# Routed experts in an order found on the chip, in pairs of a small and a large count, with slab addresses from registers

## The chip, the cores and the metric

The kernel runs on one core of a Trainium2 chip. The metric is device time in microseconds, the median of several runs. The engines are TensorE (PE in the profile, with PEld for its weight loads), VectorE (DVE), ScalarE (ACT), GpSimd (POOL) and SyncE (SP); 16 DMA engines move data for all of them.

## The reference

One decoder layer on 512 tokens of 1024 features, in float32. Three sub-layers follow each other, each with a residual and a layer norm: a gated token mixer (mLSTM and latent attention), a cross-attention into 256 memory tokens, and a mixture of experts. Only the last matters here:

```python
logits = xt @ w_router + b_router            # 512 x 32
top_val, top_idx = lax.top_k(logits, 4)      # four experts per token
gate = jax.nn.softmax(top_val)
# for each expert e, for its tokens only:
gu = x @ w_gu[e] + b_gu[e]                   # 1024 -> 2048
h  = clamped_swiglu(gu)                      # 1024
y += gate * (h @ w_dn[e] + b_dn[e])          # 1024 -> 1024
```

There are 32 experts and 2048 assignments, 64 per expert on average. Every expert has 12 MB of weights (8 MB in `w_gu`, 4 MB in `w_dn`), and every expert's weights are read once.

## The kernel before, in words

The dense part (mixer, cross-attention, router) takes the first third of the time. While its last token blocks are finished, `router_block` computes for each block of 128 tokens the logits, the top four, a 0/1 mask `M`, each token's place in its expert's list `pm` (1, 2, 3, ..., 0 where it isn't routed), the gates `G`, and for each expert the columns `VT` with the token number and the gate in bfloat16 parts. `router_end` sums the mask to the counts.

`experts` then runs over e = 0 to 32 in the order of the experts' numbers, software-pipelined over three experts at once. In iteration e TensorE does the up projection of expert e in four quarters (`up`), turns the hidden rows of expert e-1 behind the first quarter (`hidden`), makes the slot list of expert e+2 behind the third (`route_expert`), does the two halves of the down projection of expert e-1 (`down`), and between those halves turns the gathered tokens of expert e+1 (`tokens`). The order of TensorE, VectorE, ScalarE and GpSimd within this loop is written out by hand (`manual_schedule`); each engine works through its list in order.

The tokens are the stationary operand and the weights stream. What an expert costs TensorE goes by its count: 64 tokens always, 32 more if it passes 64, again 32 if it passes 96, and 64 more if it passes 128 (up to 192; beyond that `overflow`). Each of these is a branch on a register that TensorE, VectorE, ScalarE and GpSimd load from the expert's count (`number`, `conds`, line 1233). The results lie in PSUM tiles `gu` (four buffers) and `y` (two). Those of `down` use the same buffers: `y`, `y2` from `y`, and `y3`, `yx` from `gu`; `rows_out` copies them out, first the ones beyond 128, then 96 to 128, 64 to 96, and the first 64, and scatters the rows with addition into `based` in DRAM (line 1017).

The weights come as slabs of 128 x 1024 floats, 24 per expert: 16 for up, 8 for down. They go through a ring of 36 buffers. SyncE issues all of them in a fixed list (`order`, lines 1246 to 1249): up of e, then down of e-1. The first 36 are issued while the router ends; after each up projection 16 more are queued in SyncE's list, after each down projection 8 more. A slab waits on SyncE until its buffer, that of the slab 36 before, has been used.

GpSimd makes the one-hot matrix of an expert's slots from `pm` (`one_hots`, line 984), one expert ahead of its slot list, and does the gathers and scatters. The bias rows are added by a bfloat16 matmul with a selection matrix `esel`, whose column e picks expert e's row.

The lines around which the change is made:

```python
        order = []
        for e in range(33):
            order += [(e, h, k) for k in range(8) for h in range(2) if e < 32]
            order += [(e - 1, 2, k) for k in range(8) if e]
```

Of the kernel before, what the change touches and what calls it, by code (L numbers as in the profile page):

```python
# [9 lines left out]
F32 = mybir.dt.float32  # L10
F32R = mybir.dt.float32r
BF = mybir.dt.bfloat16
I32 = mybir.dt.int32
U32 = mybir.dt.uint32
AF = mybir.ActivationFunctionType
OP = mybir.AluOpType
AX = mybir.AxisListType
# [92 lines left out]
class Trunk:  # L110
# [772 lines left out]
    def router_init(self):  # L883
        nc, p, a = self.nc, self.route, self.a
        self.wr = p.tile([128, 8, 32], F32, name="wr")
        nc.gpsimd.dma_start(self.wr, a["wr"])
        self.br = p.tile([128, 32], F32, name="br")
        nc.gpsimd.dma_start(self.br, a["br"].to_broadcast([128, 32]))
        self.io32 = p.tile([128, 32], F32, name="io32")
        nc.gpsimd.iota(self.io32, pattern=[[1, 32]], base=0, channel_multiplier=0, allow_small_or_imprecise_dtypes=True)  # L890
        io = self.t2("placesf", [CAP])
        nc.gpsimd.iota(io, pattern=[[1, CAP]], base=1, channel_multiplier=0, allow_small_or_imprecise_dtypes=True)
        self.places = p.tile([128, CAP], BF, name="places")
        nc.vector.tensor_copy(self.places, io)
        self.tri = p.tile([128, 128], BF, name="tri")
        nc.vector.tensor_scalar(self.tri, self.ij, 0.0, None, op0=OP.is_gt)
        self.onesb = p.tile([128, 128], BF, name="onesb")
        nc.vector.memset(self.onesb, 1.0)
        self.M = p.tile([128, 4, 32], BF, name="M")
        self.pm = p.tile([128, 4, 32], F32, name="pm")  # L900

        self.VT = p.tile([128, 4, 32, 8], BF, name="VT")
        self.G = p.tile([128, 4, 32], F32, name="G")
        nc.gpsimd.memset(self.VT, 0.0)
        pid = p.tile([128, 1], F32, name="pid")
        nc.gpsimd.iota(pid, pattern=[[0, 1]], base=0, channel_multiplier=1, allow_small_or_imprecise_dtypes=True)
        for b in range(4):
            nc.gpsimd.tensor_copy(self.VT[:, b, :, 0], pid.to_broadcast([128, 32]))
            nc.gpsimd.memset(self.VT[:, b, :, 1], 128.0 * b - NONE)

        self.esel = p.tile([128, 32], BF, name="esel")
        e = p.tile([128, 32], F32, name="eself")
        for i in range(4):
            nc.gpsimd.iota(e[32 * i:32 * i + 32], pattern=[[1, 32]], base=0, channel_multiplier=-1,
                           allow_small_or_imprecise_dtypes=True)
        nc.vector.tensor_scalar(self.esel, e, 0.0, None, op0=OP.is_equal)
        nc.vector.memset(self.esel[96:128], 0.0)

    def router_block(self, b, x2):
# [46 lines left out]
    def router_end(self):  # L966

        nc, p = self.nc, self.route
        pc = self.ps("pc", "tp")
        for b in range(4):  # L970
            nc.tensor.matmul(pc[:, :32], self.onesb, self.M[:, b], start=b == 0, stop=b == 3)
        self.countf = p.tile([128, 32], F32, name="countf")
        nc.vector.tensor_copy(self.countf, pc[:, :32])
        self.count = p.tile([1, 32], I32, name="count")
        nc.vector.tensor_copy(self.count, pc[0:1, :32])
        self.most = p.tile([1, 1], I32, name="most")
        m = p.tile([1, 1], F32, name="mostf")
        nc.vector.reduce_max(m, pc[0:1, :32], axis=AX.X)
        nc.vector.tensor_copy(self.most, m)

    def one_hots(self, e, pool):
        oh = pool.tile([128, 4, CAP], BF, name="oh", tag="oh", bufs=1)
        for b in range(4):
            self.nc.gpsimd.tensor_scalar(oh[:, b], self.places, self.pm[:, b, e:e + 1], None, op0=OP.is_equal)  # L984
        return oh

    def route_expert(self, e, pool, oh, bank="tp"):
# [244 lines left out]
    def cond(self, c, *engines):  # L1232
        return self.nc.values_load(c[0:1, 0:1], engines=engines, min_val=0, max_val=512,
                                   skip_runtime_bounds_check_because="a count of the 512 tokens")

    def experts(self):
        nc, tc, a = self.nc, self.tc, self.a
        p, cond = self.mx, self.cond
        PE, DVE, ACT, POOL = (mybir.EngineType.PE, mybir.EngineType.DVE, mybir.EngineType.Activation, mybir.EngineType.Pool)
        self.more_x = p.tile([64, 1024], F32, name="mrxg", bufs=1)  # L1240
        nc.gpsimd.memset(self.more_x, 0.0)
        self.ys = [p.tile([128, 1024], F32, name=f"ysb{i}", bufs=1) for i in range(2)]
        for y in self.ys:
            nc.gpsimd.memset(y, 0.0)
# [5 lines that stand above are left out]
        slabs, self.nfetch = {}, 0  # L1250

        def fetch(n):

            for e, part, k in order[self.nfetch:self.nfetch + n]:
                slabs[e, part, k] = self.slab(a["wdn"][e, k] if part == 2 else a["wgu"][e, part, k])
            self.nfetch += n

        def number(e):

            c = self.mx.tile([1, 1], I32, name="number", tag="number", bufs=4)  # L1260
            nc.gpsimd.tensor_copy(c, self.count[0:1, e:e + 1])
            return c

        def conds(c):
            return cond(c, PE, ACT), cond(c, DVE, ACT), cond(c, POOL), cond(c, PE)

        def more_gather(e):
            with tc.If(rv[e][2] > 128):
                self.gather(self.more_x, route[e][1][0])

        def routing(e):
            route[e] = self.route_expert(e, self.mx, self.oh)
            if e < 31:
                count[e + 1] = number(e + 1)
                self.oh = self.one_hots(e + 1, self.mx)

        count = {0: number(0), 1: number(1)}
        route, rv, h = {0: self.first}, {0: conds(count[0])}, {}
        self.bias_rows()
        fetch(len(self.ring["s"][0]))  # L1280
        more_gather(0)
        xs, ls = {0: self.tokens(rv[0][0])}, {}
        self.oh = self.one_hots(1, self.mx)
        with tc.manual_schedule(engines={PE, DVE, ACT, POOL}):
            routing(1)
            rv[1] = conds(count[1])
            self.gather(self.xg, route[1][0][0])
            more_gather(1)
            for e in range(33):
                f = e - 1  # L1290

                def turn_units():
                    if 0 < e < 33:
                        h[f] = self.hidden(rv[f][0], *ls.pop(f))

                def next_slots():
                    if e < 30:
                        routing(e + 2)
                        rv[e + 2] = conds(count[e + 2])

                def next_tokens():
                    if e < 31:
                        xs[e + 1] = self.tokens(rv[e + 1][0])
                    if e < 30:
                        self.gather(self.xg, route[e + 2][0][0])
                        more_gather(e + 2)

                def own_units(between):
                    if e < 32:
                        ls[e] = self.units(rv[e][1], *own, route[e][2], between)  # L1310
                    else:
                        between()

                if e < 32:
                    own = self.up(rv[e][3], e, xs.pop(e), lambda h, k: slabs[e, h, k], {0: [turn_units], 2: [next_slots]})
                    fetch(16)
                else:
                    turn_units()
                if 0 < e < 33:
                    out = self.down(rv[f][3], h[f], lambda k: slabs[f, 2, k], lambda: own_units(next_tokens))  # L1320
                    fetch(8)
                    self.rows_out(rv[f][1], rv[f][2], out, route[f])
                elif e == 0:
                    own_units(next_tokens)
        self.overflow()
# [176 lines left out]
```

## Time and profile before

| what | value |
|---|---|
| time, median of 3 runs (lowest to highest) | 1847.31 us (1846.9 to 1849.73) |
| the profiled execution's own time | 1848.27 us |
| its span, first to last instruction | 1846.5 us |
| TensorE's mean granted clock | 0.977 of full speed |
| busy: PE / DVE / ACT / POOL | 1673.2 / 622.8 / 462.2 / 299.6 us |
| DMA queue q1 (all slabs): moved | 459.86 MB |
| first expert matmul to last | 632.3 to 1809.8 us |

Times in rows are microseconds from the span's start unless marked ns. A busy TensorE is not one at its peak, since its matmuls are pipelined. A float32 matmul stands in the records as two. In a timeline row the bracket holds the idle time of the engine before it, and what ended that. "PEq" and "ACTq" are the sequencers of TensorE and ScalarE, mostly a branch.

### The profile page before, as it was taken

How to read it: one execution, taken by the hardware profiler on the slowest of the kernel's cores; microseconds unless marked ns; L12 is line 12 of the kernel's file. 1: busy time of each engine (PE TensorE's matmuls, PEld its weight loads, DVE VectorE, ACT ScalarE, POOL GpSimd, SP SyncE). 2: the span in 40 equal slices, each digit the busy share in tenths (PEclk: the TensorE clock that was granted, in tenths of full speed). 3: DMA queues.
4: the chain of work that ended last, by engine and by line, in shares of the span. 5: the costliest groups of instructions: out<-in, count | busy, mean ns of one | idle time of the engine just before them, and what ended most of it. 6: DMA issues, size and time to landing. Idle time of an engine off the chain costs nothing. (4 is left out here: it accounts for less than half of the span.)

```text
span 1846.5 us, 26477 instructions
## 1 busy us (share of the span) xinstructions
PE 1673.2 (91%) x9564; PEld 855.8 (46%) x9564; DVE 622.8 (34%) x1319; ACT 462.2 (25%) x882; POOL 299.6 (16%) x413
## 2 busy tenths in 40 slices
PE   8999999999999698999999999898999999999991
PEld 6766777868987333333333333233333333333330
DVE  7854777467565421111112211111112102121114
ACT  5477655334442211101101201110101101111001
POOL 1010001421011421211101111111111211011102
PEclk9999999999999699999999999999999999999996
DMA  5223323665243699999968999999999999679963
GB/s 171 91 64 110 105 86 110 223 218 179 94 149 129 207 406 395 382 386 394 386 242 277 332 379 390 351 376 385 391 401 384 377 391 354 220 293 327 398 264 120
DMA packets 149256, 504.87 MB, mean 273 GB/s; under 512 B 21648, under 2 KB 24240, under 8 KB 149040
## 3 DMA queue, kind: packets, MB, share of 16 engines
q1 hardware_dynamic: 131632, 459.86, 66.1%
q0 software_dynamic: 17408, 42.02, 7.9%
q8 instruction: 149, 2.44, 0.5%
q14 instruction: 67, 0.55, 0.1%
HBM read 486.84 MB, written 33.29 MB: 282 GB/s over the span
## 5 line engine op out<-in xcount | busy, mean ns | idle before, releaser
L1084 PE MATMUL gu<-raw,xe 128*64 128x512 f32 (+1 forms) x2624 | 514.2, 598 | 27.5 <-issue 4.6
L1084 PEld LDWEIGHTS gu<-raw,xe 128*64 128x64 f32 (+1 forms) x2624 | 157.8, 126 | 316.4 <-issue 289.2
L1159 PE MATMUL y<-raw,hs 128*64 128x512 f32 x920 | 211.3, 597 | 17.4 <-PEq L1107 4.3
L1119 ACT ACTIVATE mg<-mg 128x512 f32<-128x512 f32 (+1 forms) x55 | 34.7, 630 | 528.3 <-DVE mg L1118 522.4
L998 DVE TENSOR_REDUCE gs<-sl 128x1 f32<-128x3 f32 x32 | 5.1, 161 | 464.8 <-PE sl L996 464.7
L984 POOL TENSOR_SCALAR oh<-places,pm 128x192 bf16<-128x192 bf16 x128 | 97.4, 790 | 381.8 <-PE sl L996 360.4
L1159 PEld LDWEIGHTS y<-raw,hs 128*64 128x64 f32 x920 | 71.7, 136 | 126.4 <-issue 89.2
L128 DVE TENSOR_TENSOR wlo<-raw,whi 128x1024 fp32r<-128x1024 f32 (+2 forms) x81 | 86.9, 1074 | 47.6 <-ACT whi L128 47.3
L1017 POOL DMA_INDIRECT based<-ysb,ixm x32 | 51.5, 1611 | 293.0 <-ACT ysb L1210 283.3
L128 ACT CAST whi<-raw 128x1024 fp32r<-128x1024 f32 (+2 forms) x81 | 75.3, 931 | 84.6 <-issue 18.6
L1084 PE MATMUL gu<-wlo,xe 128*64 128x512 f32 (+1 forms) x368 | 87.4, 594 | 3.4 <-PEq L1150 2.1
L1084 PE MATMUL gu<-whi,xe 128*64 128x512 f32 (+1 forms) x336 | 79.3, 599 | 7.6 <-PEq L1175 2.6
L1011 POOL DMA_INDIRECT xg<-x2d,ixm x32 | 36.0, 1124 | 305.9 <-PEq L1068 178.1
L1118 DVE TENSOR_SCALAR mg<-gu 128x512 f32<-128x512 f32 (+1 forms) x52 | 35.8, 688 | 127.5 <-PE gu L1076 125.4
L1065 ACT COPY xe<-xt 128x512 f32<-128x512 f32 x50 | 27.8, 587 | 194.2 <-PE xt L1056 193.6
L1166 PE MATMUL y<-raw,hs 128*32 128x512 f32 x440 | 57.6, 598 | 0.0
L1197 DVE TENSOR_TENSOR ysb<-ysb,y 32x512 f32<-32x512 f32 x30 | 20.4, 681 | 103.4 <-ACT ysb L1196 103.3
L160 PE MATMUL g<-xTh,wlo 128*128 128x512 f32 x128 | 52.7, 411 | 2.8 <-DVE wlo L128 2.8
L1144 ACT COPY hs<-ht 128x512 f32<-128x512 f32 (+1 forms) x55 | 26.5, 509 | 104.5 <-PEq L1148 52.8
L158 PE MATMUL g<-xTh,whi 128*128 128x512 f32 x128 | 52.4, 410 | 0.0
L159 PE MATMUL g<-xTl,whi 128*128 128x512 f32 x128 | 52.0, 406 | 0.0
L1084 PEld LDWEIGHTS gu<-wlo,xe 128*64 128x64 f32 (+1 forms) x368 | 25.1, 125 | 50.0 <-issue 48.1
(494 smaller groups left out, 2779.8 us busy)
## 6 DMA issues: line engine op xcount, KB each, us to landing
raw<-in_wgu SPq DMA_DIRECT2D x406, 512.0 KB
raw<-in_wdn SPq DMA_DIRECT2D x230, 512.0 KB
wlo<-in_wgu SPq DMA_DIRECT2D x53, 512.0 KB
whi<-in_wgu SPq DMA_DIRECT2D x53, 512.0 KB
raw<-in_wt SPq DMA_DIRECT2D x27, 512.0 KB
whi<-in_wdn SPq DMA_DIRECT2D x13, 512.0 KB
wlo<-in_wdn SPq DMA_DIRECT2D x13, 512.0 KB
tgd<-tg POOLq DMA_DIRECT2D x16, 256.0 KB, 3.7
```

Source lines behind the costliest of these rows:

```text
L128: return nc.scalar.copy(hi, src).ins, (lo_eng or nc.vector).tensor_sub(lo, src, hi.bitcast(F32)).ins
L158: mm(out, w[0], x[0], start=start, stop=False)
L159: mm(out, w[0], x[1], start=False, stop=False)
L160: mm(out, w[1], x[0], start=False, stop=stop)
L984: self.nc.gpsimd.tensor_scalar(oh[:, b], self.places, self.pm[:, b, e:e + 1], None, op0=OP.is_equal)
L1011: return self.nc.gpsimd.indirect_dma_start(out=xg, out_offset=None, in_=self.x2d, in_offset=bass.IndirectOffsetOnAxis(ap=ix[:, 0:1], axis= ...
L1017: self.nc.gpsimd.indirect_dma_start(out=self.based, out_offset=bass.IndirectOffsetOnAxis(ap=ix[:, 0:1], axis=0), in_=y, in_offset=None, bo ...
L1084: mm(out(h, j), x[:, k], w(h, k)[:, ts(j, 512)], start=k == 0, stop=False)
L1118: nc.vector.tensor_scalar(g, pg, 7.0, None, op0=OP.min)
L1119: nc.scalar.activation(g, g, AF.Gelu_apprx_sigmoid)
L1159: self.nc.tensor.matmul(o[64 * n:64 * n + 64], h[:, k], w(k)[:, ts(n, 512)], start=k == 0, stop=k == 7)
L1166: self.nc.tensor.matmul(o[r:r + 32], h[:, k], w(k)[:, ts(n, 512)], start=k < 2, stop=k > 5)
```

## The change

The kernel no longer takes the experts by number but by position. Positions 0 and 1 are experts 0 and 1. The other 30 are ranked by count on the chip (rank 2 the largest, 31 the smallest, ties by number), and a fixed table gives each position its rank: 17, 16, 18, 15, 19, 14, 20, 13, 21, 12, and then 31, 2, 30, 3, 29, 4, 28, 5, 27, 6, 26, 7, 25, 8, 24, 9, 23, 10, 22, 11.

`order_experts`, called in `router_end`, forms a key of 32 times the count and the number, along a row and along a column, counts for each expert how many keys are greater, and compares that rank with the table: a 0/1 matrix `P` of experts by positions. It also goes into `esel`. `place_experts`, called once behind the tokens of expert 0, turns `pm` and `G`, multiplies them with `P` and so permutes their columns into `pmp` and `VT`, and does the same with the experts' numbers and counts (`placed`). From position 1 on `one_hots` and `number` read these. For a slab from position 2 on, SyncE loads the expert's number into a register, once per expert, and the slab's DRAM address is worked out from that.

```diff
-        nc.vector.tensor_scalar(self.esel, e, 0.0, None, op0=OP.is_equal)
+        nc.vector.tensor_scalar(e, e, 0.0, None, op0=OP.is_equal)
...
+        for i in range(4):
+            for b in range(4):
+                nc.tensor.matmul(pc[32 * i:32 * i + 32, 32:33], self.M[:, b], self.onesb[:, 0:1], start=b == 0, stop=b == 3)
+        self.order_experts(pc)
...
+    def order_experts(self, pc):
...
+        for q, n, i, d in ((0, 5, 14, -1), (5, 10, 0, 1)):
+            for at, base, step in ((2, 31 - i, -d), (3, 2 + i, d)):
+                nc.gpsimd.iota(rank[:, at + 2 * q:at + 2 * (q + n) - 1:2], pattern=[[step, n]], base=base, channel_multiplier=0,
+                               allow_small_or_imprecise_dtypes=True)
+        nc.gpsimd.memset(rank[:, 0:1], 0.0)
+        nc.gpsimd.memset(rank[:, 1:2], 1.0)
+
+        nc.gpsimd.iota(first, pattern=[[-1, 32]], base=0, channel_multiplier=0, allow_small_or_imprecise_dtypes=True)
+        nc.gpsimd.memset(first[:, 0:1], 65536.0)
+        nc.gpsimd.memset(first[:, 1:2], 32768.0)
+        nc.vector.scalar_tensor_tensor(row, pc[:, :32], 32.0, first, op0=OP.mult, op1=OP.add)
+        nc.vector.tensor_copy(self.countc, pc[:, 32:33])
+        t = self.P
+        nc.vector.tensor_mul(t, self.eself, first)
+        nc.vector.reduce_sum(key, t, axis=AX.X)
+        nc.vector.scalar_tensor_tensor(key, self.countc, 32.0, key, op0=OP.mult, op1=OP.add)
+        nc.vector.tensor_scalar(t, row, key, None, op0=OP.is_gt)
+        nc.vector.reduce_sum(r, t, axis=AX.X)
+        nc.vector.tensor_scalar(self.P, rank, r, None, op0=OP.is_equal)
+        nc.vector.tensor_copy(self.esel[0:96], self.P[0:96])
+        self.eidx = p.tile([32, 2], F32, name="eidx")
+        nc.gpsimd.iota(self.eidx[:, 0:1], pattern=[[0, 1]], base=0, channel_multiplier=1, allow_small_or_imprecise_dtypes=True)
+
+    def place_experts(self):
...
+        for i, src in enumerate((self.pm, self.G)):
+            pt = self.ps("plt", "tp")
+            for b in range(4):
+                nc.tensor.transpose(pt[:32, ts(b, 128)], src[:, b], self.ident)
+            nc.scalar.copy(T[i], pt[:32])
+        o = self.ps("plo", "tp")
+        for i in range(2):
+            for b in range(4):
+                nc.tensor.matmul(o[:, ts(4 * i + b, 32)], T[i][:, ts(b, 128)], self.P[0:32], start=True, stop=True)
+        n = self.ps("pln", "tp")
+        nc.tensor.matmul(n[0:1, 0:32], self.eidx[:, 0:1], self.P[0:32], start=True, stop=True)
+        nc.tensor.matmul(n[0:1, 32:64], self.countc[0:32], self.P[0:32], start=True, stop=True)
...
+        nc.vector.tensor_copy(self.placed, n[0:1, 0:64])
...
+        nc.vector.tensor_copy(self.pmp.rearrange("p b e -> p (b e)"), o[:, 0:128])
...
+        nc.vector.tensor_copy(g, o[:, 128:256])
+        out = self.VT.rearrange("p b e c -> p (b e) c")[:, :, 2:5]
+        nc.vector.tensor_copy(out[:, :, 0], g)
...
-            self.nc.gpsimd.tensor_scalar(oh[:, b], self.places, self.pm[:, b, e:e + 1], None, op0=OP.is_equal)
+            self.nc.gpsimd.tensor_scalar(oh[:, b], self.places, (self.pmp if e else self.pm)[:, b, e:e + 1], None, op0=OP.is_equal)
...
-            for e, part, k in order[self.nfetch:self.nfetch + n]:
-                slabs[e, part, k] = self.slab(a["wdn"][e, k] if part == 2 else a["wgu"][e, part, k])
+            for p, part, k in order[self.nfetch:self.nfetch + n]:
+                if p > 1 and p not in expert:
+                    expert[p] = nc.sync.value_load(self.placed[0:1, p:p + 1], min_val=0, max_val=31)
+                e = ds(expert[p], 1) if p > 1 else slice(p, p + 1)
+                src = a["wdn"][e, k] if part == 2 else a["wgu"][e, part, k]
+                slabs[p, part, k] = self.slab(src.rearrange("o p n -> (o p) n"))
...
-            nc.gpsimd.tensor_copy(c, self.count[0:1, e:e + 1])
+            nc.gpsimd.tensor_copy(c, self.placed[0:1, 32 + e:33 + e] if e else self.count[0:1, 0:1])
...
-        count = {0: number(0), 1: number(1)}
+        count = {0: number(0)}
...
         xs, ls = {0: self.tokens(rv[0][0])}, {}
+        self.place_experts()
+        count[1] = number(1)
         self.oh = self.one_hots(1, self.mx)
```

## Rows read from the trace of the kernel before

**Rows 1.** The page, parts 1 and 2: whole program.
```profile
...
PE 1673.2 (91%) x9564; PEld 855.8 (46%) x9564; DVE 622.8 (34%) x1319; ACT 462.2 (25%) x882; POOL 299.6 (16%) x413
...
DMA  5223323665243699999968999999999999679963
...
```

**Rows 2.** Windows: us, busy us of each engine (count), clock, DMA share, GB/s.
```profile
...
688.00:866.00 178.00, 161.69 (x1010) 57.42 (x1012) 27.23 (x61) 19.08 (x35) 30.44 (x36) 1.00 1.01 389
930.00:1010.00 80.00, 74.73 (x506) 25.49 (x504) 17.60 (x34) 8.93 (x16) 8.88 (x11) 1.00 0.71 250
1293.00:1463.00 170.00, 154.16 (x912) 55.08 (x908) 27.58 (x61) 18.75 (x33) 31.62 (x39) 1.00 1.02 390
...
```

**Rows 3.** Waits of SyncE, 640 to 1780: total us, times, longest us.
```profile
...
SPq L184 <- DMA raw<-in_wgu: 248.9, 254, 3.3
...
```

**Rows 4.** Waits of TensorE's weight loads, 640 to 1800, same columns.
```profile
...
PEld gu L1084 <- DMA raw<-in_wgu: 17.0, 36, 1.4
...
```

**Rows 5.** DMA, 541 to 688: queue, packets, MB, share; issues with KB each.
```profile
...
q1 hardware_dynamic: 9014, 30.23, 55.5%
...
based<-x SPq DMA_DIRECT2D x8, 256.0 KB
...
x2d<-x SPq DMA_DIRECT2D x2, 256.0 KB
...
```

**Rows 6.** DMA, 688 to 866.
```profile
...
q1 hardware_dynamic: 17995, 65.52, 93.7%
...
```

**Rows 7.** DMA, 1293 to 1463.
```profile
...
q1 hardware_dynamic: 17304, 63.01, 94.8%
...
```

**Rows 8.** Timeline of TensorE, 687 to 760: start us, us, engine, line, operation.
```profile
...
687.96 1.94 PE L1084 MATMUL gu<-whi,xe 128*64 128x512 f32 x8 [0.31 <-PEq L1175]
...
```

**Rows 9.** Timeline of TensorE, 1231 to 1362: first matmuls of experts 17 to 20.
```profile
...
1266.49 1.94 PE L1084 MATMUL gu<-whi,xe 128*64 128x512 f32 x8 [0.30 <-PEq L1175]
...
1280.58 3.65 PE L1084 MATMUL gu<-raw,xe 128*64 128x512 f32 x16 [0.30 <-issue]
...
1284.97 3.65 PE L1159 MATMUL y<-raw,hs 128*64 128x512 f32 x16 [0.30 <-DMA wlo<-in_wdn]
...
1298.02 3.65 PE L1084 MATMUL gu<-raw,xe 128*64 128x512 f32 x16 [0.66 <-ACT ysb L1196]
...
1325.01 5.51 PE L1084 MATMUL gu<-raw,xe 128*64 128x512 f32 x32 [0.31 <-PEq L1175]
...
1360.71 1.51 PE L1084 MATMUL gu<-whi,xe 128*64 128x512 f32 x6 [0.31 <-PEq L1175]
```

**Rows 10.** Timeline, 1578 to 1600: expert 24's last add, 26's matmuls.
```profile
...
1588.52 0.68 DVE L1197 TENSOR_TENSOR ysb<-ysb,yx 32x512 f32<-32x512 f32 x1 [0.64 <-ACT ysb L1196]
...
1589.35 1.06 PE L1084 MATMUL gu<-whi,xe 128*32 128x512 f32 x8 [2.13 <-DVE ysb L1197]
...
```

**Rows 11.** Timeline, 1758 to the end: scatters of experts 29 and 31.
```profile
...
1773.28 1.92 PE L1166 MATMUL y<-raw,hs 128*32 128x512 f32 x16
...
1780.27 1.56 POOL L1017 DMA_INDIRECT based<-ysb,ixm  x1 [32.10 <-ACT ysb L1210]
...
1807.01 2.77 PE L1159 MATMUL y<-raw,hs 128*64 128x512 f32 x12
...
1811.39 1.56 POOL L1017 DMA_INDIRECT based<-ysb,ixm  x1 [7.91 <-ACTq L1332]
...
```

**Rows 12.** GpSimd's groups by line, 480 to 632: shapes, count, busy us, mean ns.
```profile
...
L892 POOL IOTA placesf<- 128x192 f32 x1 | 0.3, 302 | 66.0 <-PE cpt L801 66.0
```

**Rows 13.** Timeline of all engines, 600 to 636: how the experts start.
```profile
...
628.46 2.99 POOL L984 TENSOR_SCALAR oh<-places,pm 128x192 bf16<-128x192 bf16 x4
...
632.34 4.07 PE L1084 MATMUL gu<-raw,xe 128*64 128x512 f32 x9
...
```

**Rows 14.** Line 1233, register loads: ns min/median/max, first and last start us.
```profile
...
L1233 POOLq TENSOR_LOAD <-number x32: 292/298/523, 621.8 to 1714.1; - x32
...
```

**Rows 15.** Line 184 on SyncE, slab issues: same columns.
```profile
...
L184 SPq DMA_DIRECT2D raw<-in_wdn x230: 327/328/1274, 654.0 to 1777.9; - x115
...
```

More of the change, by code (lines that the diff above doesn't have):

```diff
@@ L911, in router_init @@
         self.esel = p.tile([128, 32], BF, name="esel")
-        e = p.tile([128, 32], F32, name="eself")
+        e = self.eself = p.tile([128, 32], F32, name="eself")
         for i in range(4):
@@ L979, in router_end @@
         nc.vector.tensor_copy(self.most, m)
+    def order_experts(self, pc):
+        nc, p = self.nc, self.route
+        t = self.t2("oe")
+        row, rank, first = [t[:, ts(i, 32)] for i in range(3)]
+        self.P = p.tile([128, 32], F32, name="P")
+        self.countc = p.tile([128, 1], F32, name="countc")
+        key, r = [p.tile([128, 1], F32, name="oe" + n) for n in ("key", "r")]
+        for q, n, i, d in ((0, 5, 14, -1), (5, 10, 0, 1)):
[19 more added lines that the diff above has]
+        nc.gpsimd.iota(self.eidx[:, 0:1], pattern=[[0, 1]], base=0, channel_multiplier=1, allow_small_or_imprecise_dtypes=True)
@@ new lines, in place_experts @@
+    def place_experts(self):
+        nc, p = self.nc, self.mx
+        T = [p.tile([128, 512], F32, name=n, tag=n, bufs=1)[:32] for n in ("ml2", "mlx")]
+        for i, src in enumerate((self.pm, self.G)):
[10 more added lines that the diff above has]
+        nc.tensor.matmul(n[0:1, 32:64], self.countc[0:32], self.P[0:32], start=True, stop=True)
+        self.placed = self.route.tile([1, 64], I32, name="placed")
+        nc.vector.tensor_copy(self.placed, n[0:1, 0:64])
+        self.pmp = p.tile([128, 4, 32], F32, name="pmp", bufs=1)
+        nc.vector.tensor_copy(self.pmp.rearrange("p b e -> p (b e)"), o[:, 0:128])
+        t = p.tile([128, 512], F32, name="Gp", tag="mg", bufs=1)
+        g, r = t[:, 0:128], t[:, 128:256]
+        nc.vector.tensor_copy(g, o[:, 128:256])
+        out = self.VT.rearrange("p b e c -> p (b e) c")[:, :, 2:5]
+        nc.vector.tensor_copy(out[:, :, 0], g)
+        nc.vector.tensor_sub(r, g, out[:, :, 0])
+        nc.vector.tensor_copy(out[:, :, 1], r)
+        nc.vector.tensor_sub(out[:, :, 2], r, out[:, :, 1])
@@ L1252, in fetch @@
         def fetch(n):
-            for e, part, k in order[self.nfetch:self.nfetch + n]:
-                slabs[e, part, k] = self.slab(a["wdn"][e, k] if part == 2 else a["wgu"][e, part, k])
+            for p, part, k in order[self.nfetch:self.nfetch + n]:
[4 more added lines that the diff above has]
+                slabs[p, part, k] = self.slab(src.rearrange("o p n -> (o p) n"))
             self.nfetch += n
+        expert = {}
         def number(e):
             c = self.mx.tile([1, 1], I32, name="number", tag="number", bufs=4)
-            nc.gpsimd.tensor_copy(c, self.count[0:1, e:e + 1])
+            nc.gpsimd.tensor_copy(c, self.placed[0:1, 32 + e:33 + e] if e else self.count[0:1, 0:1])
             return c
```

## The prediction, made before the change was run

> **What bounds the kernel now.** I read the page first: TensorE is busy for 91% of the span, and from slice 14 on, where the experts run, the row of the DMA engines also stands mostly at 9 [rows 1]. So two resources could set the time. The stretches tell which: the transfers are full (share 1.01 and 1.02, 389 and 390 GB/s) from 688 to 866 and from 1293 to 1463 us, and half idle (0.71, 250 GB/s) from 930 to 1010, but TensorE works at about the same pace in all three (161.7 of 178, 154.2 of 170 and 74.7 of 80 us) [rows 2]. The waits decide it. SyncE, which issues the weight slabs, waits 248.9 us for earlier slabs of `in_wgu` to land [rows 3], yet TensorE's weight loads wait for such slabs only 36 times, 17.0 us together, at most 1.4 us [rows 4]. The 36-slab ring is what lies between: TensorE sets the time, and the ring hides the transfers. The expert time is the sum of TensorE's work, which depends on how many of the limits 64, 96 and 128 each count passes. A sum doesn't change with the order. So the change can win only the little that the ring doesn't hide, and it can lose by letting the ring run dry.
>
> **The order.** From the reference's inputs I worked out the 32 counts. By the diff's rank table the positions hold, as expert counts: 49, 68 (experts 0 and 1), then 52, 58, 50, 65, 49, 67, 45, 72, 45, 73, then 9, 147, 15, 144, 21, 131, 22, 119, 27, 117, 31, 94, 36, 85, 38, 83, 41, 80, 42, 73. Before, experts 1 to 8 are 68, 94, 45, 50, 119, 41, 117, 131: heavy, so the slabs gain on TensorE. After, the start is light.
>
> **Part 1, slab supply at the start.** A slab is 128 x 1024 floats, 0.524 MB. Queue q1 moves 65.52 MB in the 178 us from 688, which is 125.0 slabs or 1.424 us each [rows 6], and 63.01 MB in 170 us later, 1.415 us each [rows 7]; I take 1.42, so 34.1 us for an expert's 24 slabs. When TensorE starts position 2 at 687.96 [rows 8], q1 has moved 30.23 MB since 541, of which eight and two writes of 0.262 MB are no slabs [rows 5]: 27.6 MB, 52.7 slabs. It needs number 40 then. Positions 0 and 1 are unchanged, so the new order starts from the same 12.7 slabs of lead.
>
> How long TensorE takes from one expert's first matmul to the next one's follows from experts 17 to 20 [rows 9], whose counts are 22, 27, 67 and 85: a count up to 64 behind one over 64 takes 1298.02 - 1266.49 = 31.5 us, up to 64 behind up to 64 takes 27.0, over 64 behind up to 64 takes 35.7. Positions 2 to 11 are then 31.5 + 27.0 + 27.0 + 35.7 and three times (31.5 + 35.7) = 322.8 us, so position 12 would start at 1010.8 and, 14.1 us on (1280.58 - 1266.49), its last quarter at 1024.9. The 16 slabs of that up projection end at number 295. Then comes position 11's down projection, numbers 296 to 303; its first half wants the first 300 slabs by about 1032.0: 4.4 us for the quarter with its bias (1284.97 - 1280.58), and three quarters of the half's 3.65. The transfers have them at 688 + (300 - 52.7) x 1.42 = 1039.2. TensorE must have waited 7.2 us by then: three light positions in a row eat the lead, and each further pair (67.2 us against 68.2) eats one more. At 1.38 us a slab the wait is nothing; at 1.45 it is 15. Behind it comes the count of 147, whose work refills the ring. The last five pairs, again about 67 us each, live off a full ring. I take **+8**, a little more for restarting behind each wait, bounds 0 and +15.
>
> **Part 2, accumulator pile-up.** When the expert two back passed 128, its many result copies are still running when the next one's 32-wide matmuls want that accumulator. It is seen once now, at expert 26 (147) behind 24 (144): the VectorE add that frees it ends at 1589.20, and TensorE starts at 1589.35, 2.13 us late [rows 10]. In the new order 144 follows 147, 131 follows 144 and 119 follows 131, each two positions later: three times, net 2 x 2.13 = **+4.3**, bounds 0 (if something else holds TensorE there) and +7.
>
> **Part 3, the end.** The last expert is now one of 73 rows, not 36. From the last matmul to the issue of its scatter: for an expert over 64 it is 1780.27 - 1775.20 = 5.1 us, for the present last one 1811.39 - 1809.78 = 1.6 [rows 11]. Nothing hides it: **+3.5**, bounds +3 and +6, since more rows are also scattered.
>
> **Part 4, the start.** GpSimd gets ten iotas and memsets, 0.3 us for one iota in the trace [rows 12], before its clears and the bias loads: 2 to 3 us. VectorE's chain in `order_experts` is nine short operations, and TensorE's transposes and 32-column products stand behind the first tokens, where TensorE waits for the one-hots until 628.46 anyway [rows 13]. So the first up matmul moves from 632.34 by 1 to 4 us; I take 2. In these the slabs go on landing, so Part 1 shrinks by as much: beside it the start costs **0**; without it, its 2.
>
> **Part 5, addresses from registers.** One register load per expert and address arithmetic per slab on SyncE. Register loads on GpSimd take 0.298 us [rows 14]; a slab's issue takes 0.328 of its 1.42 us [rows 15]. No row shows address arithmetic; the nearest bounds are 0 and a few such loads, 1 us, per slab, and up to that SyncE's own wait for landings [rows 3] covers it, so **0**; if more, the last rival. The per-expert gathers, one-hots and scatters are the same number of instructions on other columns: 0.
>
> **Sum:** 8 + 4.3 + 3.5 = +16 on the profiled 1848.27 us (span 1846.5), so 1864.1; the median of the runs is 1.0 lower, hence 1863 to 1864. I say 1864.
>
> **Rivals.** (a) The slabs keep up: the pitch falls to 1.38 because the early experts gather and scatter fewer rows. Then 2 + 4.3 + 3.5: 1857. For it: TensorE's waits make room; against: the later stretch has light experts too and still shows 1.415. Chance 0.22. (b) Faster: part of TensorE's busy time in the full-DMA stretches is really waiting for slabs. Busy there is 0.908, in the half-idle stretch 0.934 [rows 2]. If the 0.026 over some 850 us were such waiting, evening out the demand would return 22 us, and with the 10 us of the other parts the time would be 1835. It decides as soon as more than 10 us were hidden. Against it: the 12.7 slabs of lead at 688, and waits of 17.0 us in all [rows 4]. Chance 0.07. The Trainium skill, "Perfetto Trace Analysis", section "Optimization Strategy" (under Identifying Performance Opportunities), says that a kernel whose busiest engine changes over time may gain by interleaving the regimes; the transfers here do alternate [rows 2], but TensorE leads in both, so the trace doesn't bear the rule out. (c) The order on the chip isn't the one that I computed, or the ring never drains and the copies overlap: within 1844 to 1851. Chance 0.07. (d) SyncE can't issue every 1.42 us because of the register arithmetic: position 2's first slab is issued eight after 654.0 [rows 15], so near 665; at 1.65 us each its 720 slabs end at 1853, where now the last is issued at 1777.9. The last matmul is then near 1863, and with 37 us behind it, as now, and Part 2 and 3 the time is near 1905. Chance 0.06.
>
> **Numbers.** The forecast itself has 0.58, with a range of its own from 1858 to 1874. With (a), and some excess in Parts 2 to 4, 1850 to 1880 holds 0.8. Some 0.2%, 3.7 us, is what a measurement tells from no change. Slower: forecast, (a) and (d), 0.86; same 0.07; faster 0.07.
>
> **What would show it.** Right: TensorE waits for slabs, together 5 to 12 us, at positions 4 to 12 only, with the transfers full without a break from 640 to about 1040; gaps of 2 us in the first quarter of positions 15, 17 and 19; the last scatter 5 us behind the last matmul. Wrong: slab waits past position 13, SyncE's slabs more than 1.42 us apart without waiting, or an expert phase shorter than the present 1177 us from 632 to 1809 [rows 11, 13].

## The result, and the profile after

The changed kernel takes 1874.35 us (1871.46 to 1875.14), the one before 1847.11 us beside it (1846.24 to 1849.73): a ratio of 1.014, 95% interval 1.0126 to 1.0154. It is slower, as forecast, and inside the range of 1850 to 1880, but just beyond the forecast's own range, which ended at 1874: it lost 27 us where the sum said 16.

The profiled executions (1875.14 and 1848.27 us) differ by as much, and their spans divide in three. The first up matmul starts 3.2 us later (635.54 for 632.34). From there to the end of the last matmul, which I call the expert phase, it takes 1197.5 us for 1177.4: +20.1. Behind it come 40.3 us for 36.7: +3.6.

First parts 1 and 2 of the page of after, which answer [rows 1]. Counted from 0, the DMA row now stands at 9 from slice 14 to 23, where the light experts run, and lower in most of the next six.

```profile
PE 1695.1 (90%) x9608; PEld 864.0 (46%) x9608; DVE 626.6 (33%) x1335; ACT 463.5 (25%) x884; POOL 301.9 (16%) x423
...
DMA  5223324675243799999999998684979899999933
```

The windows of after, columns as in [rows 2]: from 691.6 to 1040 us, positions 2 to 12, the transfers are full without a break. TensorE is busy for 0.901 of that; the stretch of full transfers before gave 0.908.

```profile
640.00:688.00 48.00, 43.72 (x274) 15.80 (x272) 12.39 (x28) 10.06 (x13) 9.70 (x13) 0.99 1.03 407
691.60:1040.00 348.40, 313.97 (x1784) 111.01 (x1784) 49.96 (x115) 35.47 (x63) 61.71 (x73) 1.00 1.01 383
```

The DMA queue of the slabs in two windows of after, 541 to 775.3 and 691.6 to 1040 us (packets, MB, share). The second line is 242.6 slabs of 0.524 MB in 348.4 us, or 1.436 us each; [rows 6] and [rows 7] gave 1.424 and 1.415.

```profile
q1 hardware_dynamic: 17711, 61.88, 69.7%
...
q1 hardware_dynamic: 34928, 127.18, 94.0%
```

What TensorE's weight loads and matmuls wait for in after, 620 to 1846 us (total us, times, longest us), which answers [rows 4]; the last two lines are the kernel before, in the same window. The weight loads' total grew from 17.0 to 24.4 us and the longest from 1.4 to 2.1. The matmuls' own waits say where the rest is: before, their up projections waited 2.3 us for `raw` slabs, never for `whi`, and once, 2.1 us, for the VectorE add of `rows_out`. Now they wait 7.0 us for `raw` and 2.6 for `whi`, and for that add three times.

```profile
PEld gu L1150 <- DMA raw<-in_wgu: 24.4, 46, 2.1
...
PE gu L1150 <- DMA raw<-in_wgu: 7.0, 15, 1.2
PE gu L1150 <- DVE ysb L1263: 6.4, 3, 2.1
...
PE gu L1150 <- DMA whi<-in_wgu: 2.6, 7, 0.8
```

```profile
PE gu L1084 <- DMA raw<-in_wgu: 2.3, 7, 0.5
PE gu L1084 <- DVE ysb L1197: 2.1, 1, 2.1
```

The timeline of TensorE in after, around the starts of positions 2 to 5, and the start of position 12. Positions 2 to 5 begin at 691.57, 722.84, 749.13 and 780.10 us. The steps 31.3 and 26.3 are still those of [rows 9]; the third, 31.0 where 27.0 was counted, holds the first waits for slabs.

```profile
691.57 1.94 PE L1150 MATMUL gu<-whi,xe 128*64 128x512 f32 x8 [0.30 <-DMA raw<-in_wdn]
...
722.84 3.65 PE L1150 MATMUL gu<-raw,xe 128*64 128x512 f32 x16 [0.56 <-PEq L1243]
...
749.13 3.65 PE L1150 MATMUL gu<-raw,xe 128*64 128x512 f32 x16 [0.30 <-DMA raw<-in_wgu]
...
759.90 2.36 PE L1150 MATMUL gu<-raw,xe 128*64 128x512 f32 x8 [1.19 <-DMA raw<-in_wgu]
762.47 1.93 PE L1150 MATMUL gu<-raw,xe 128*64 128x512 f32 x6 [0.22 <-DMA raw<-in_wgu]
...
780.10 1.04 PE L1150 MATMUL gu<-whi,xe 128*64 128x512 f32 x2 [0.31 <-DMA whi<-in_wgu]
781.91 1.93 PE L1150 MATMUL gu<-whi,xe 128*64 128x512 f32 x6 [0.77 <-DMA whi<-in_wgu]
...
1025.47 3.65 PE L1150 MATMUL gu<-raw,xe 128*64 128x512 f32 x16 [0.30 <-PEq L1241]
```

Against the median times that the same pairs of neighbouring pieces of work take in the trace before, positions 4 to 12 hold about 15.6 us of such waits: some 4 at each of positions 4 and 5, then about 2 at the light positions 6, 8 and 12 and 1 at 10. From position 13 on there are none. A second reading agrees: from position 2 to position 12 it takes 1025.47 - 691.57 = 333.9 us, where those medians sum to 320.4; that is 13.5 before position 12, and 2.0 in it.

The first 32-wide matmuls of positions 15, 17 and 19 in after, as in [rows 10]: the same 2.13 us gap, three times. Below them stand windows just behind the three gaps, columns as in [rows 2]. Behind the first two the granted clock is 0.50, the 1.2 GHz level; behind the third it stays 1.00.

```profile
1163.36 4.91 PE L1150 MATMUL gu<-raw,xe 128*32 128x512 f32 x28 [2.13 <-DVE ysb L1263]
...
1264.96 1.07 PE L1150 MATMUL gu<-whi,xe 128*32 128x512 f32 x8 [2.13 <-DVE ysb L1263]
...
1366.22 3.64 PE L1150 MATMUL gu<-raw,xe 128*32 128x512 f32 x32 [2.14 <-DVE ysb L1263]
```

```profile
1164.00:1166.00 2.00, 2.00 (x16) 0.75 (x12) 1.32 (x3) 0.58 (x1) 0.00 (x0) 0.50 0.12 47
1267.00:1269.00 2.00, 2.00 (x13) 0.55 (x9) 1.93 (x3) 0.00 (x0) 0.00 (x0) 0.50 0.00 0
1366.00:1368.00 2.00, 1.78 (x20) 0.72 (x24) 1.50 (x3) 0.39 (x1) 0.00 (x0) 1.00 0.18 72
```

The end in after, answering [rows 11]: the last matmuls run until 1831.62 + 1.46 = 1833.08, the scatter is issued at 1838.15, 5.07 us later. Between them ScalarE and VectorE copy the rows above 64 in turn.

```profile
1821.61 1.94 PE L1225 MATMUL y<-whi,hs 128*64 128x512 f32 x8 [0.83 <-ACT hs L1210]
...
1831.62 1.46 PE L1232 MATMUL y<-raw,hs 128*32 128x512 f32 x10
...
1833.15 0.58 ACT L1262 COPY ysb<-y 32x512 f32<-32x512 f32 x1 [11.32 <-PE y L1232]
...
1838.15 1.55 POOL L1083 DMA_INDIRECT based<-ysb,ixm  x1 [15.38 <-ACTq L1406]
```

The start in after, answering [rows 13]: the products of `place_experts` hold TensorE until 630.3, VectorE writes the parts of `VT` until 633.6, and TensorE's slot list waits 3.11 us for it. It then waits once more, until 634.68, for the last of the one-hots: GpSimd could begin them only at 631.11, behind `pmp`, where before it began at 628.46.

```profile
626.72 1.91 PE L1030 MATMUL plo<-P,ml 32*128 32x32 f32 x8
...
628.45 1.89 PE L1030 MATMUL plo<-P,mlx 32*128 32x32 f32 x8
...
630.37 0.29 DVE L1037 COPY pmp<-plo 128x128 f32<-128x128 f32 x1 [8.07 <-PE plo L1030]
...
631.11 3.52 POOL L1050 TENSOR_SCALAR oh<-places,pmp 128x192 bf16<-128x192 bf16 x4
...
632.87 0.73 DVE L1045 TENSOR_TENSOR VT<-Gp,VT 128x128 bf16<-128x128 f32 x1
...
633.75 0.39 PE L1059 MATMUL sl<-VT,oh 128*128 128x8 bf16 x3 [3.11 <-DVE VT L1045]
...
634.68 0.50 PE L1059 MATMUL sl<-VT,oh 128*128 128x8 bf16 x5 [0.55 <-POOL oh L1050]
...
635.54 1.97 PE L1150 MATMUL gu<-raw,xe 128*64 128x512 f32 x4
```

### The profile page after: what moved, and what is told of

It is laid out like the page before. It is cut to its first block, busy times and chain, and to the rows that moved or that the text cites. A ratio compares the mean times of both kernels' runs of the same rounds, so it can differ in the third digit from the quotient of the medians.

```text
span 1873.4 us, 28125 instructions
## 1 busy us (share of the span) xinstructions
PE 1695.1 (90%) x9608; PEld 864.0 (46%) x9608; DVE 626.6 (33%) x1335; ACT 463.5 (25%) x884; POOL 301.9 (16%) x423
## 5 line engine op out<-in xcount | busy, mean ns | idle before, releaser
L1150 PE MATMUL gu<-raw,xe 128*64 128x512 f32 (+1 forms) x2664 | 526.9, 602 | 32.7 <-DMA raw<-in_wgu 5.3
L1050 POOL TENSOR_SCALAR oh<-places,pmp 128x192 bf16<-128x192 bf16 x124 | 94.5, 771 | 369.9 <-PE sl L1062 369.9
L1150 PE MATMUL gu<-whi,xe 128*64 128x512 f32 (+1 forms) x332 | 83.5, 615 | 9.4 <-DVE ysb L1263 2.1
L1150 PE MATMUL gu<-wlo,xe 128*64 128x512 f32 (+1 forms) x332 | 82.7, 606 | 2.9 <-PEq L1216 0.5
L1150 PEld LDWEIGHTS gu<-wlo,xe 128*64 128x64 f32 (+1 forms) x332 | 24.6, 128 | 46.6 <-issue 40.3
```

What stands on the lines that cost most here:

```text
L1050: self.nc.gpsimd.tensor_scalar(oh[:, b], self.places, (self.pmp if e else self.pm)[:, b, e:e + 1], None, op0=OP.is_equal)
L1150: mm(out(h, j), x[:, k], w(h, k)[:, ts(j, 512)], start=k == 0, stop=False)
```

## The experiments

**Order or machinery?** The first two part the order from what finds it. `e1_static` keeps the order and compiles it into SyncE's list, with no register load and no computed address (`ORDER` is the list of the experts' numbers):

```diff
...
-                if p > 1 and p not in expert:
-                    expert[p] = nc.sync.value_load(self.placed[0:1, p:p + 1], min_val=0, max_val=31)
-                e = ds(expert[p], 1) if p > 1 else slice(p, p + 1)
+                e = slice(ORDER[p], ORDER[p] + 1)
```

> The changed kernel in the same order, but with the experts' numbers written into the program: no register loads and no address arithmetic on SyncE; the ordering on the chip stays. If the order itself costs the time (light experts first, three counts over 128 two positions apart): 1873 to 1875, TensorE's slab waits as in the changed kernel. If SyncE's addresses from registers slow the slabs: the pitch from 690 to 1040 us falls from 1.436 to 1.42 or below, and the time to 1858 to 1868.

Measured 1873.25 us, a ratio of 1.0135 to the kernel before, with its 95% interval [1.0113, 1.0157] (so too below): nothing comes back that the intervals could tell. The queue in its window of positions 2 to 12:

```profile
q1 hardware_dynamic: 34977, 127.36, 94.4%
```

That is 1.434 us a slab with constant addresses, 1.436 with computed ones. `e2_identity` keeps all the machinery and the old order:

```diff
-        nc.vector.tensor_scalar(self.P, rank, r, None, op0=OP.is_equal)
+        nc.vector.tensor_scalar(self.P, self.eself, 1.0, None, op0=OP.is_equal)
```

> The changed kernel with all its machinery, but the table replaced so that every position gets the expert of its own number: the old order, with addresses from registers. If the order costs the time: only the start remains, 1850 to 1852 (first up matmul at 635.5 instead of 632.3, and 1 us more at the lower clock). If the machinery costs it: 1865 to 1875.

Measured 1849.12 us, 1.0004 [0.9992, 1.0016]. Its first up matmul comes 16.2 us behind the start of the count's matmuls (after 16.3, `e1_static` 16.2, before 12.9); its expert phase is 1175.3 us, 2.1 shorter than before. So the start does cost 3 us in the trace and the median moves by 1.8, inside its interval. The loss is the order's.

**Slab supply.** `e3_heavy_first` starts with the extreme pairs, the large one first, and ends with the middle ones:

```diff
-        for q, n, i, d in ((0, 5, 14, -1), (5, 10, 0, 1)):
-            for at, base, step in ((2, 31 - i, -d), (3, 2 + i, d)):
+        for q, n, i, d in ((0, 10, 0, 1), (10, 5, 14, -1)):
+            for at, base, step in ((2, 2 + i, d), (3, 31 - i, -d)):
```

> The changed kernel with another table: the extreme pairs first and the larger count first in each pair (147, 9, 144, 15, 131, 21, 119, ...), the middle pairs last, ending on a count of 45. If the slabs run dry because the early positions are light: the 15.6 us of slab waits go and the end is 3.5 us shorter, the three pile-ups of 10 us stay: 1853 to 1858. If the waits have another cause, such as addresses or the ordering work: 1868 to 1872.

Measured 1862.28 us, 1.0082 [1.0057, 1.0106], above what was expected. The waits for slabs at the start went: from 691.6 to 1040 us TensorE's matmuls wait once for a slab, 0.4 us, where after has

```profile
PE gu L1150 <- DMA raw<-in_wgu: 5.1, 11, 1.2
PE gu L1150 <- DMA whi<-in_wgu: 2.3, 6, 0.8
```

Its expert phase (1189.3 us) is 7.4 us longer than after's less the 15.6. The expectation left out 5.7 us at the last expert (45 rows behind 73), which `e6_tail` below shows more plainly. The pile-ups cost 2.6, 2.6 and 3.9 us, 9.1 together, a little less than priced. Some 2.6 us stay without a cause. `e4_fewer_slabs` keeps after's order and leaves out the down slabs of two positions, so its output isn't the layer's:

```diff
...
-            order += [(e - 1, 2, k) for k in range(8) if e]
+            order += [(e - 1, 2, k) for k in range(8) if e and e - 1 not in (2, 3)]
...
```

> The changed kernel without the 16 down slabs of positions 2 and 3: their down projections use the next position's up slabs, so the transfers have 23 us less to do early on, and TensorE's work is the same in number. If supply is what TensorE waits for at positions 4 to 12, all 15.6 us of it go: 1857 to 1861. If the waits aren't supply: 1872 to 1875.

Measured 1859.07 us, 1.0057 [1.0036, 1.0078]; expert phase 1182.0, 15.5 less than after. The same two rows in its trace, 691.6 to 1040:

```profile
PE gu L1150 <- DMA raw<-in_wgu: 0.7, 2, 0.5
...
PE gu L1150 <- DMA whi<-in_wgu: 0.4, 1, 0.4
```

Sixteen slabs fewer return as much as the 15.6 us read from the trace. The order loses more than half of what it loses to the ring.

**Pile-up.** `e5_pile` is after with two blocks of `rows_out` exchanged: for a count over 128 the rows 96 to 128, whose accumulator is wanted next, are copied ahead of the rows beyond:

```diff
             with tc.If(rv > 96):
+                sums(slice(96, 128), p[2])
                 with tc.If(rv > 128):
...
-                sums(slice(96, 128), p[2])
```

> The changed kernel with one block of rows_out moved: rows 96 to 128 are copied out ahead of those beyond 128, so the accumulator that the expert two positions on wants is free 2.6 us after the down projection and not 5.6. If the gaps in the first quarter of positions 15, 17 and 19 (2.15 us each, with 3.1 us more behind them) are this pile-up: they go, 1864 to 1867. If something else holds TensorE there: 1873 to 1875.

Measured 1864.11 us, 1.0086 [1.0071, 1.0101], 10.2 less than after. The timeline of TensorE in it, position 15: the 48 matmul records of the first quarter on `gu`, and the 16 on `gux`, follow without a gap.

```profile
1155.81 7.17 PE L1150 MATMUL gu<-raw,xe 128*64 128x512 f32 x48
1162.91 3.65 PE L1150 MATMUL gux<-raw,xe 128*64 128x512 f32 x16
```

From their first matmul to the transposes behind them, the first quarters of positions 15, 17 and 19 take 10.69, 10.69 and 7.73 us in it, where after takes 14.59, 14.59 and 9.93: 10.0 less. Its expert phase is only 8.7 less (1188.9); by the reckoning of the slab waits above it waits about 2.5 us more for slabs than after.

**The end.** `e6_tail` exchanges the last two positions, so that 42 rows are last, behind 73:

```diff
         nc.gpsimd.memset(rank[:, 1:2], 1.0)
+        nc.gpsimd.memset(rank[:, 30:31], 11.0)
+        nc.gpsimd.memset(rank[:, 31:32], 22.0)
```

> The changed kernel with the last two positions swapped: 73 rows, then 42. If the end is longer because the last expert has rows beyond 64: from the last matmul to the last scatter 1.6 us instead of 5.1, so 1870.5 to 1871.5. If the tail doesn't depend on it: 1874 to 1875.

Measured 1878.26 us, 1.0164 [1.0148, 1.0179]: slower than after, against the expectation. What lies behind the last matmul did fall, from 40.3 to 36.9 us; but the expert phase rose by 6.8. The timeline of `e6_tail` at the end, and below it its windows (TensorE is idle from 1821.7 to 1825.99):

```profile
1820.60 0.58 ACT L1264 COPY ysb<-y 32x512 f32<-32x512 f32 x1 [10.72 <-PE y L1234]
...
1824.74 0.58 ACT L1278 COPY ysb<-y 64x512 f32<-64x512 f32 x1 [2.25 <-DVE ysb L1277]
1825.35 0.58 ACT L1212 COPY hs<-ht 128x512 f32<-128x512 f32 x1
...
1825.99 3.68 PE L1227 MATMUL y<-whi,hs 128*64 128x512 f32 x8 [4.25 <-ACTq L1216]
...
1829.45 3.06 PE L1227 MATMUL y<-wlo,hs 128*64 128x512 f32 x8
```

```profile
1820.00:1824.00 4.00, 1.19 (x12) 0.42 (x4) 2.11 (x3) 1.15 (x2) 0.00 (x0) 1.00 0.00 0
1824.00:1826.00 2.00, 0.01 (x2) 0.02 (x2) 0.68 (x1) 1.17 (x2) 0.40 (x1) 0.75 0.00 0
1826.00:1830.00 4.00, 4.00 (x10) 1.23 (x12) 0.00 (x0) 0.00 (x0) 1.15 (x1) 0.50 0.43 56
1830.00:1834.00 4.00, 3.84 (x15) 1.06 (x13) 0.00 (x0) 0.00 (x0) 0.00 (x0) 0.77 0.15 32
```

ScalarE works in order: it copies out the 73 rows of the expert before (1820.60 to 1825.32) before it copies the last expert's hidden rows, which TensorE waits for: 4.25 us, where after waits 0.83. Behind that idle stretch the granted clock is 0.50, the 1.2 GHz level, and the first 16 matmul records take 3.68 + 3.06 us where after, at a granted clock of 1.00, takes 1.94 and 1.89. The longer wait and the slower matmuls are 3.4 + 2.9 = 6.3 of the 6.8 us; the rest wasn't taken apart.

**A better order?** `e8_before_pile` is the kernel before with the exchanged blocks of `e5_pile` alone. `e10_mixed_pile` has those blocks and a third table, heavy and middle pairs by turns (147, 9, 58, 52, 144, 15, ... 80, 41, 73, 42):

```diff
...
+        for at, by, n, base, step in ((2, 4, 5, 2, 1), (3, 4, 5, 31, -1), (4, 4, 5, 16, -1), (5, 4, 5, 17, 1),
+                                      (22, 2, 5, 7, 1), (23, 2, 5, 26, -1)):
...
```

> The kernel before with the same block of rows_out moved. It has one such gap, 2.13 us at expert 26 with 0.4 behind it: if it is the pile-up, 1844.3 to 1845.3, else 1847.

> The changed kernel with a third table, heavy and middle pairs by turns, the larger count first (147, 9, 58, 52, 144, 15, 65, 50, 131, ...), ending on 42, and the moved block of rows_out. If order acts only through slab supply, pile-up and tail, all three are gone and 1844 to 1847 is left, no better than the order by number; if pairing small and large counts itself gains something, it would be below 1843.

Measured 1844.33 us, 0.9985 [0.9975, 0.9996], and 1851.78 us, 1.0019 [1.0008, 1.0029]. The second misses, by the same end as `e6_tail`, 42 rows last behind 73: TensorE waits 4.26 us there. `e11_small_end` is the same with 80, 73, 41, 42 at the end, and `e12_before_pile_again` repeats `e8_before_pile` beside it:

```diff
...
+        nc.gpsimd.memset(rank[:, 29:30], 11.0)
+        nc.gpsimd.memset(rank[:, 30:31], 23.0)
...
```

> The third table and the moved block as in the run before, with the last four positions 80, 73, 41, 42 instead of 80, 41, 73, 42. If the end is long because ScalarE copies out the 73 rows before it can copy the last expert's hidden rows (TensorE waits 4.2 us for that and then runs 7 us at half its clock): both go, and the last matmul comes 6 us earlier, 1845 to 1847. If the end is long because of the slabs or of the last expert's own count: 1851 to 1853, as in the run before.

> The kernel before with the moved block of rows_out once more, beside the run above, to tell which of the two is ahead: 1844 to 1845 if its first result holds.

Measured 1846.70 us, 0.9990 [0.9979, 1.0001], and 1844.54 us, 0.9980 [0.9968, 0.9991]. In `e11_small_end` the wait at the last expert is short and the matmul behind it at full pace:

```profile
1799.76 1.94 PE L1227 MATMUL y<-whi,hs 128*64 128x512 f32 x8 [1.22 <-ACTq L1216]
```

Its expert phase is 1173.0 us, the shortest of all, 4.4 below before; but 3 of that go at the start. The best version is the kernel before with two blocks exchanged, 3 us (0.2%) faster than before in both of its runs. The gap of [rows 10] is gone from its traces: the first quarter of expert 26 takes 10.69 us in both, 13.30 before. Their expert phases are yet 1178.0 and 1177.8 us, because other stretches of these two executions were longer than in the one profiled before. The largest is at expert 9: 32 matmul records take 7.09 and 7.20 us for 5.51, at a granted clock of 0.76 from 985 to 990 in `e8_before_pile`, where before has 1.00. What lowered the clock there isn't shown.

## Why the prediction was right, and where its sum was too small

**What bounds the kernel: right.** TensorE sets the time and the ring hides the transfers, so an order can win little and lose by draining the ring. Of the orders run, those that start light pay for slabs, and the best of the other new orders stands at 0.9990, with the exchanged blocks in it. But the time fell into the range because the range was 30 us wide. The sum is 11 us short, and both of its larger parts came out just beyond their upper bounds (15.6 for +15, 7.4 for +7). Of the signs named, the places were as said; the 5 to 12 us of slab waits were not.

**Part 1, +8 with the start in it: right in kind, too small.** The waits begin at position 4 and end at position 12, with the transfers full throughout, but they sum to 15.6 us, and `e4_fewer_slabs` confirms the size. The term that failed is the supply, "52.7 slabs" landed at 688 and 1.42 us each. Bytes that have moved in sum are not slabs that may be used. By the first line of the queue, 61.88 MB had moved in after by 775.3 us; less ten writes of 0.262 MB that is 113.0 slabs, enough for position 5, which begins with the 113th. TensorE starts it at 780.10, and at 780.07 SyncE issues the slab eight further on. SyncE's list holds a slab back not only until its buffer is free, but also until the slab eight before has landed (the waits of [rows 3]): eight are in flight, and the oldest is complete only then, 4.8 us behind the byte count. The issue, in SyncE's timeline of after:

```profile
780.07 0.33 SPq L184 DMA_DIRECT2D raw<-in_wgu  x1
```

In the trace before SyncE had issued 58 by 688, so that by the same reading 50 and not 52.7 were ready; 2.7 x 1.43 is 3.9 us. The pitch of 1.436 instead of 1.42 over 247 slabs adds 4.0, and the ten steps, 320.4 instead of 322.8 us by the medians of the trace before, 2.4. The later start gives 3.6 back. 7.2 + 3.9 + 4.0 + 2.4 - 3.6 = 13.9 for the waits up to slab 300, position 12's among them. Most of what is missing to 15.6 is that by these terms slab 300 would be there at 688 + 250 x 1.436 = 1047.0, while in after SyncE issues the slab eight further on at 1048.26.

**Part 2, +4.3: right in place, too small.** The gaps are at positions 15, 17 and 19, 2.13 us each. But against `e5_pile` the three quarters lose 3.9, 3.9 and 2.2 us, 10.0 together; net of the one before, which cost 2.6, that is 7.4. The sum had nothing for what follows a gap: behind the first two the granted clock fell to 0.50, and the 32 matmul records of the 32-wide matmuls took 5.3 us, where behind the third, at 1.00, they took 3.64. The clock doesn't always fall: in `e1_static` and `e6_tail`, with the same work at position 15, it stays 1.00 behind the same gap, and the quarter takes 13.31 us and not 14.59. What decides it isn't shown. `e5_pile` returns 10.2.

**Part 3, +3.5: right** as read (5.07 for 1.61 us). But it isn't a loss that another last expert avoids at will: `e6_tail` takes it away and pays twice as much ahead of it.

**Part 4, counted 0 beside Part 1: the size right, the cause wrong.** The start moved by 3.2 us, in the bounds of 1 to 4, and the reckoning of Part 1 above needs the 3.6 us that the slabs gained by it; no run shows this return by itself. What TensorE waits for is not what was named. GpSimd's iotas delay nothing: its bias loads end at 628.29, before at 628.42. The prediction took the products of `place_experts` to lie hidden behind the wait for the one-hots. But the one-hots now need `pmp`, and that comes out of these 16 small float32 products (3.6 us), as `VT` does.

**Part 5, addresses: right.** Register operations, address move and issue on SyncE in after (ns min/median/max, first and last start):

```profile
L184 SPq FUSED_REGOPS  x720: 4/46/250, 664.7 to 1786.7; - x180
...
L184 SPq DMA_DIRECT2D raw<-in_wdn x230: 327/333/940, 654.0 to 1787.6; - x115
L184 SPq MOVE raw<-in_wdn x215: 29/29/37, 722.3 to 1787.5; - x108
```

46 + 29 + 5 ns beside the 328 of [rows 15] still fit three times into a slab's 1.43 us. `e1_static`, where the issue takes 328 ns and has neither of the other two, returns nothing, and rival (d) falls.

**Sum:** 3.2 + 15.6 + 7.4 + 3.5 = 29.7, less the 2.1 us by which the phase of `e2_identity` is shorter than before, 27.6; the spans differ by 26.9. These are single executions, and the kernel before alone ran from 1843.62 to 1852.59 us, so the agreement to 1 us is in part luck.

**The rivals.** (a) fell: the pitch was longer than 1.42, not shorter. (b) fell: in `e11_small_end` the heavy-and-middle order evens the demand out (DMA share 0.90 to 0.97 in four stretches from 640 to 1800 us, before 0.84 to 1.02), and the phase is 4.4 us shorter, far from 22. The exchanged blocks are worth 2.6 of that, and the phase of `e2_identity`, in the old order, is 2.1 shorter as well. The rule of the Trainium skill ("Perfetto Trace Analysis", "Optimization Strategy") that interleaving may gain where the most-contended engine changes over time finds nothing to gain here: the up projections of the kernel before waited 2.3 us for `raw` slabs in all, so there was no stretch in which the transfers led. The rule's condition wasn't met. (c) fell: the ring drained and the gaps stand at the positions that were worked out.

## What to carry to other kernels

Here one engine sets the time and a ring hides the transfers, and the order of work items won nothing by balance. It acted through three places: how fast the ring drains at the start, which item is behind which on a shared accumulator, and what the last two items leave uncovered. Count a transfer as usable when its semaphore comes, not when the bytes add up: where, as here, the issue of a transfer waits for the one n before it, that is when the one n further on is issued. Price a gap on TensorE with the matmuls behind it, since the granted clock may fall: 2.13 us of waiting cost 2.2 to 3.9. Before an order is changed around a wait, look whether two blocks exchanged in the engine that makes it take the wait away: here that was the only gain.

## What was not expected of the hardware

A slab was complete 4.8 us after the sum of bytes reached it, with eight in flight on 16 engines and 1.43 us between completions. An idle stretch of 4.25 us on TensorE, at a granted clock of 1.00 until 1824 and 0.75 in the last 2 us, was followed by 4 us at 0.50 and 4 at 0.77, which cost 2.9 us beside the wait itself. A gap of 2.13 us was followed by 0.50 in some places and by 1.00 in others, even at the same position of the same order. A DMA address computed in registers cost SyncE some 80 ns per transfer.
